# A hybrid decoder layer: the transposed keys are copied out of PSUM after the scores, and the idle products at the start read a smaller tile

## The chip, the cores and the metric

The kernel runs on one core of a Trainium2 chip. The metric is the device time of one execution in microseconds; before the change its median is 398.11 us in three runs (397.14 to 398.34).

## The reference, cut to what matters

One layer of a decoder, for 1024 prompt tokens and 64 sample tokens (8 sequences of 8), width 1024, float32. One input projection feeds two groups of heads; each is gated, both are concatenated, mapped by one output projection, and a layer norm ends the layer.

```python
proj = jnp.einsum('btd,de->bte', x, w_in)
u, gp, q, k, v, gg, fa = jnp.split(proj, SPLIT_IDX, axis=-1)
pool_out, new_buf = pool_mix(u, buf, start_pos, w_map, pool_scale)      # trailing windows 2/4/8/16
...
def step(S, inp):                                   # gated linear attention, one block of tokens
    qb, kb, vb, gb = inp
    b = jnp.cumsum(gb, axis=2)
    inter = jnp.einsum('bhck,bhkv->bhcv', qb * jnp.exp(b), S)
    ...
    A = jnp.einsum('bhtk,bhsk,bhtsk->bhts', qb, kb, decay)              # the scores, masked
    intra = jnp.einsum('bhts,bhsv->bhtv', A, vb)
    S_new = jnp.exp(bC)[..., None] * S + jnp.einsum('bhsk,bhsv->bhkv', kb * jnp.exp(bC[:, :, None] - b), vb)
    return S_new, inter + intra
...
mix = jnp.concatenate([pool_out * jax.nn.silu(gp), o.astype(x.dtype) * jax.nn.silu(gg)], axis=-1)
y = jnp.einsum('bte,ed->btd', mix, w_out)
h = (DEEPNORM_ALPHA * x + y).astype(jnp.float32)    # then the layer norm
```

## The kernel before

Every large product is taken three times over operands that are split into a rounded high part and a rest (`split`, lines 59 to 64; `mm3`, lines 66 to 70: high times high, high times rest, rest times high). The tokens stand in three pieces of 384, 384 and 320 columns.

The program has four stretches, each written out in the order in which the engines run it. First come the value projections (`v_group`, products named psv): the first three token tiles are worked with the contraction outermost, so that each piece of x and of the weights is used as soon as ScalarE and VectorE have split it (lines 309 to 318). Then 16 weight tiles, each over the three token pieces (`group`, products psm, 24 of them for one piece). After each piece `tick` runs what is due: `later` queues a step with a due slot, and slots count pieces. The steps of the gated linear attention are queued in this way (lines 432 to 440), one set for each of eight blocks of 128 prompt tokens (c = 0 to 7) and one for the 64 sample tokens (c = 8). Last come the output projection and the layer norm (`out_tile`, products pso).

For a prompt block c the steps due in one slot are, in this order: `s1a` of block c, `s2p` of block c-1, `s1b` of block c, `s2` of block c-1; `s3` of block c-1 follows one slot later. `s1a` transposes the keys of the block (two products pskt, line 724) into the first 256 columns of a PSUM bank called `pk`, and ScalarE copies them to SBUF as `kt` (line 726). `s2p` multiplies kt of the block before by its values (psp_, line 766). `s1b` computes the scores of the four heads (line 735): two heads go to the last 256 columns of the same bank (`pa[0]`, shown as pskt), two go to a second bank (psa). VectorE multiplies both by the mask into `am` (line 737). `s2` multiplies am of the block before by the values (line 804) and adds the queries times the state (line 802). `kt` of block c is read by `s2p` of block c one block later, and `am` of block c by `s2` of block c one block later. The squares of the output, their split and the sum over the ones (psms, line 833) follow in `s2` and `s3`. In the slot of block 0 there is no `s2p` and no `s2`, and in that of the sample block they are absent too.

Ahead of all this, GpSimd clears some tiles (lines 180 to 186), among them `warm`, 128 by 512; TensorE then multiplies this tile by itself nine times (line 189, psw), with a result that nobody reads, until the first pieces of x and of the weights are there. SyncE's queue issues the loads, the first at 0.73 us.

A second body, `Body(..., True)`, is run only when a flag says that the decay is too strong for the short form of the scores. It does not run with these inputs.

Of the kernel before, what the change touches and what calls it, by code (L numbers as in the profile page):

```python
# [7 lines left out]
F32 = mybir.dt.float32  # L8
FR = mybir.dt.float32r
I32 = mybir.dt.int32  # L10
ALU = mybir.AluOpType
AF = mybir.ActivationFunctionType
# [27 lines left out]
class Body:  # L40
# [54 lines left out]
    def emit(self):  # L95
        self.cms = {}
        tc, nc, io, safe = self.tc, self.nc, self.io, self.safe
# [32 lines left out]
        et = self.pool("et", 2)  # L130
# [46 lines left out]
                (nc.scalar if k == 0 and n == 0 else nc.sync).dma_start(raw, src)  # L177
        rst = ep.tile([128, 384], F32, name="rst")
        rst2 = ep.tile([128, 320], F32, name="rst2")
        nc.gpsimd.memset(wa2r, 0.0)  # L180
        nc.gpsimd.memset(sel, 0.0)
        nc.gpsimd.memset(eps[:, 0:1], RMS_EPS)
        nc.gpsimd.memset(eps[:, 1:2], LN_EPS)
        nc.scalar.preload_act_table_set(EXP_LN)
        warm = et.tile([128, 512], F32, tag="ab", name="warm")
        nc.gpsimd.memset(warm, 0.0)
        psw = psg.tile([128, 512], F32, tag="g", name="psw")
        for _ in range(9):
            nc.tensor.matmul(psw, warm[:, :128].bitcast(FR), warm.bitcast(FR), start=True, stop=True)  # L189


        order = [("k", 0), ("k", 1), ("q", 0), ("q", 1)]
# [362 lines left out]
        for j, t in enumerate(OUT_ORDER):  # L555
# [9 lines left out]
            if j in (4, 6):  # L565
                p = j // 2 - 2
# [115 lines left out]
    def gla_steps(self, c):  # L682
        nc, gl = self.nc, self.glp
        sample = c == 8
        t0, n = (128 * c, 128) if not sample else (NP, NS)
        K, Q = self.K[:, :, t0:t0 + n], self.Q[:, :, t0:t0 + n]
        msk = self.smask if sample else self.mask
        st = {}
# [3 lines left out]
        def g_tile(name):  # L692
            return self.psg.tile([128, 512], F32, tag="g", name=name)
# [14 lines left out]
        def s1():  # L708
            s1a()
            s1b()  # L710

        def s1a():
            Kst, Qi = K, Q
            am = gl.tile([128, 4, 128], F32, tag="am", bufs=1 if self.safe else 2, name="am")
            st["am"] = am
            if self.safe:
                Kst, Qi = self.safe_scores(c, am, t0, n, sample)
            st["Qi"] = Qi
            if sample and not self.safe:
                Kst = st["kd"]  # L720
            pk = g_tile("pskt")
            pa = [pk[:, 256:], None]
            for p in range(2):
                nc.tensor.transpose(pk[:n, p * 128:(p + 1) * 128], Kst[:, p], self.ident)
            kt = self.kt8 if sample else gl.tile([128, 256], F32, tag="kt", bufs=1 if self.safe else 2, name="kt")
            nc.scalar.activation(kt[:n], pk[:n, :256], AF.Copy)
            st["kt"], st["pa"] = kt, pa

        def s1b():
            am, pa, Qi = st["am"], st["pa"], st["Qi"]  # L730
            if not self.safe:
                pa[1] = g_tile("psa1")
                for h in range(4):
                    r, p = rows[h % 2], h // 2
                    nc.tensor.matmul(pa[h % 2][:n, p * n:(p + 1) * n], K[r, p], Q[r, p], start=True, stop=True)  # L735
                for e in range(2):
                    nc.vector.tensor_tensor(am[:n, two(e), :n], pa[e][:n, :2 * n].rearrange("s (p t) -> s p t", p=2),
                                            msk[:n, :n].unsqueeze(1).broadcast_to([n, 2, n]), op=ALU.mult)
            if sample:
                qb = gl.tile([128, 2, NB, 4, SEG], F32, tag="shl", bufs=1, name="qb")  # L740
                nc.gpsimd.memset(qb, 0.0)
                for p in range(2):
                    for h in range(2):
                        nc.vector.tensor_copy(qb[rows[h], p, :, h, :],
                                              Qi[rows[h], p].rearrange("k (b s) -> k b s", b=NB))
                st["qb"] = qb
# [108 lines left out]
        if sample:  # L855
            return [s0, s0k, s1, sample_inter, s2, s3]
        return [s1, s2, s3] if self.safe else [s1a, s1b, s2p, s2, s3]


# [174 lines left out]
```

## Time and profile before

| | us |
|---|---|
| median of three runs | 398.11 |
| the profiled execution | 397.98 |
| its span, first to last instruction | 396.2 |
| VectorE busy | 217.7 |
| ScalarE busy | 143.6 |
| values and gates, to about | 58 |
| first weight tiles, to about | 110 |
| weight tiles with the attention steps, to about | 222 |

A row of the timeline reads: start and duration in us, engine, line, operation, out<-in, the tile sizes, and in brackets the time that the engine stood idle before it with what released it. PE rows are TensorE's products, PEld rows are its weight loads, which run ahead of the products. A row of the view of waits reads: engine, what waited, line, what it waited for, then the time in total, how often, and the longest.

### The profile page before, as it was taken

To read this page: it belongs to the slowest core of one execution; us is meant where nothing else is said; L and a number is where in the kernel's file an instruction comes from. 1 tells how busy PE (TensorE), PEld (TensorE's weight loads), DVE (VectorE), ACT (ScalarE), POOL (GpSimd) and SP (SyncE) were. 2 spreads that over 40 slices of the span, in tenths; PEclk is the share of its full clock that TensorE was granted. 3 is DMA by queue.
4 is the path that set the end of the run, shared out by engine and by line. 5 is a ranking of instruction groups with operands and counts; after the bars stand their busy time and mean duration, and the time that the engine had idled before them with its cause. 6 is when DMAs were issued, how large, how long until landed. Compare 5 with 4: busy or idle time off the path is not lost.

```text
span 396.2 us, 6088 instructions
## 1 busy us (share of the span) xinstructions
PE 383.3 (97%) x2473; PEld 358.3 (90%) x2473; DVE 217.7 (55%) x429; ACT 143.6 (36%) x273; POOL 8.6 (2%) x31
## 2 busy tenths in 40 slices
PE   8999999999999999999999999999999999999991
PEld 7999999999989999999899899999988888888790
DVE  4775555621354778788433321333399565556683
ACT  5554554410023425435766222421283333211200
POOL 1000000000000000000001000100000000000000
PEclk9999999999999999999999999999999999999996
DMA  7960001011100101030103110443330253242321
GB/s 257 393 237 2 19 36 55 3 51 53 55 19 36 53 2 52 3 141 20 55 0 97 53 37 17 161 160 101 132 141 10 96 213 106 108 159 79 103 84 60
DMA packets 11556, 34.29 MB, mean 87 GB/s; under 512 B 1776, under 2 KB 3232, under 8 KB 11264
## 3 DMA queue, kind: packets, MB, share of 16 engines
q1 hardware_dynamic: 10960, 32.24, 23.7%
q0 software_dynamic: 416, 1.46, 1.1%
q8 instruction: 21, 0.34, 0.3%
q10 hardware_dynamic: 144, 0.14, 0.1%
q14 instruction: 15, 0.12, 0.1%
HBM read 27.91 MB, written 5.91 MB: 85 GB/s over the span
## 4 chain that ended last, share of the span: by engine, by line
PE 93%; ACT 3%; issue 1%; DVE 1%; POOL 0%; ACTq 0%; POOLq 0%
PE psm L68 15%; PE psm L69 15%; PE psm L70 15%; PE pso L68 7%; PE pso L69 7%; PE pso L70 7%; PE psv L69 4%; PE psv L68 4%; PE psv L70 4%; PE pskt L735 1%; PE psw L189 1%; PE pso L75 1%; PE pso L78 1%; PE pso L804 1%; PE psms L833 1%
## 5 line engine op out<-in xcount | busy, mean ns | idle before, releaser
L68 PE MATMUL psm<-xc,hl 128*128 128x384 f32 (+1 forms) x384 | 126.2, 329 | 0.0
L70 PE MATMUL psm<-xc,hl 128*128 128x384 f32 (+1 forms) x384 | 125.4, 327 | 0.0
L69 PE MATMUL psm<-xc,hl 128*128 128x384 f32 (+1 forms) x384 | 125.3, 326 | 0.0
L68 PEld LDWEIGHTS psm<-xc,hl 128*128 128x128 f32 x384 | 72.1, 188 | 0.7 <-issue 0.2
L69 PEld LDWEIGHTS psm<-xc,hl 128*128 128x128 f32 x384 | 72.2, 188 | 0.1
L70 PEld LDWEIGHTS psm<-xc,hl 128*128 128x128 f32 x384 | 72.1, 188 | 0.0
L68 PE MATMUL psv<-wv,xc 128*128 128x264 f32 x128 | 36.9, 288 | 0.0
L70 PE MATMUL psv<-wv,xc 128*128 128x264 f32 x128 | 36.7, 287 | 0.0
L69 PE MATMUL psv<-wv,xc 128*128 128x264 f32 x128 | 36.7, 286 | 0.0
L68 PE MATMUL pso<-wo,mx 128*128 128x512 f32 (+1 forms) x85 | 32.0, 377 | 0.0
L70 PE MATMUL pso<-wo,mx 128*128 128x512 f32 (+1 forms) x85 | 32.0, 377 | 0.0
L69 PE MATMUL pso<-wo,mx 128*128 128x512 f32 (+1 forms) x85 | 32.0, 377 | 0.0
L539 ACT ACTIVATE mv<-mv,eps 128x1 f32<-128x1 f32 (+1 forms) x9 | 2.7, 295 | 64.8 <-DVE mv L538 64.8
L403 DVE SCALAR_TENSOR_TENSOR vm<-sg,vecs,vm 128x128 f32<-128x128 f32 (+1 forms) x36 | 10.3, 340 | 27.8 <-ACT sg L397 27.8
L64 DVE TENSOR_TENSOR hl<-raw,hl 128x1024 fp32r<-128x1024 f32 x19 | 23.2, 1223 | 3.8 <-ACT hl L61 3.5
L644 ACT ACTIVATE ue<-psm 128x384 f32<-128x384 f32 (+1 forms) x12 | 5.5, 456 | 53.4 <-PE psm L70 49.5
L68 PEld LDWEIGHTS psv<-wv,xc 128*128 128x128 f32 x128 | 24.6, 192 | 0.1
L69 PEld LDWEIGHTS psv<-wv,xc 128*128 128x128 f32 x128 | 24.5, 191 | 0.1
L532 DVE SCALAR_TENSOR_TENSOR hh<-xr,pso 128x512 f32<-128x512 f32 (+2 forms) x19 | 12.4, 654 | 21.8 <-PE pso L70 21.6
L70 PEld LDWEIGHTS psv<-wv,xc 128*128 128x128 f32 x128 | 24.4, 190 | 0.0
L61 ACT ACTIVATE hl<-raw 128x1024 fp32r<-128x1024 f32 x19 | 19.9, 1051 | 6.4 <-PE psm L70 6.4
L68 PE MATMUL pso<-hl,mx 128*128 128x512 f32 (+1 forms) x51 | 19.3, 379 | 0.0
(236 smaller groups left out, 587.3 us busy)
## 6 DMA issues: line engine op xcount, KB each, us to landing
raw<-wm_dram SPq DMA_DIRECT2D x16, 512.0 KB, 3.5
xr<-x_dram SPq DMA_DIRECT2D x8, 512.0 KB, 4.3
o_y_dram<-hh SPq DMA_DIRECT2D x7, 512.0 KB, 2.9
wr<-w_out_dram SPq DMA_DIRECT2D x5, 512.0 KB, 4.5
s<-s_dram SPq DMA_DIRECT2D x2, 1024.0 KB, 6.7
hl<-xt_dram SPq DMA_DIRECT2D x2, 768.0 KB, 7.0
raw<-w_out_dram SPq DMA_DIRECT2D x3, 512.0 KB, 3.4
hl<-xt_dram SPq DMA_DIRECT2D x2, 640.0 KB, 5.4
```

The costliest lines, as they stand in the source:

```text
L61: self.nc.scalar.activation(hi.bitcast(FR), raw, AF.Copy)
L64: (on_lo or self.nc.vector).tensor_tensor(lo.bitcast(FR), raw, hi, op=ALU.subtract)
L68: nc.tensor.matmul(ps, ahi.bitcast(FR), bhi.bitcast(FR), start=first, stop=False)
L69: nc.tensor.matmul(ps, ahi.bitcast(FR), blo.bitcast(FR), start=False, stop=False)
L70: nc.tensor.matmul(ps, alo.bitcast(FR), bhi.bitcast(FR), start=False, stop=last)
L75: one = lambda st, sp: nc.tensor.matmul(ps, both.bitcast(FR), bhi.bitcast(FR), start=st, stop=sp)
L78: nc.tensor.matmul(ps[:64], both[:, :64].bitcast(FR), blo.bitcast(FR), start=False, stop=False)
L189: nc.tensor.matmul(psw, warm[:, :128].bitcast(FR), warm.bitcast(FR), start=True, stop=True)
L403: nc.vector.scalar_tensor_tensor(pg, sg[:, to:to + tn], self.norm[:, m:m + 1], pg, op0=ALU.mult, op1=ALU.mult)
L532: nc.vector.scalar_tensor_tensor(hh[:n, s], x[:n, s], ALPHA if n == 128 else 1.0, ps[h][:n, :wd], op0=ALU.mult, op1=ALU.add)
L644: nc.scalar.activation(ue[:, HIST:HIST + np_], src[:, :np_], AF.Copy)
L735: nc.tensor.matmul(pa[h % 2][:n, p * n:(p + 1) * n], K[r, p], Q[r, p], start=True, stop=True)
```

## The change

It has two parts. `warm` becomes 128 by 128, is cleared by GpSimd ahead of the other tiles, and the nine products read it four times over as a moving operand of 512 columns (an access that returns to the first column after each 128). And the copy of the transposed keys, `kt`, is taken out of `s1a` into a function `keys`, which `s1b` calls after the score products; in the second body it stays where it was.

```diff
         rst2 = ep.tile([128, 320], F32, name="rst2")
+        warm = et.tile([128, 128], F32, tag="ab", name="warm")
+        nc.gpsimd.memset(warm, 0.0)
         nc.gpsimd.memset(wa2r, 0.0)
         nc.gpsimd.memset(sel, 0.0)
         nc.gpsimd.memset(eps[:, 0:1], RMS_EPS)
         nc.gpsimd.memset(eps[:, 1:2], LN_EPS)
         nc.scalar.preload_act_table_set(EXP_LN)
-        warm = et.tile([128, 512], F32, tag="ab", name="warm")
-        nc.gpsimd.memset(warm, 0.0)
         psw = psg.tile([128, 512], F32, tag="g", name="psw")
+        wide = warm.bitcast(FR).unsqueeze(1).broadcast_to([128, 4, 128])
         for _ in range(9):
-            nc.tensor.matmul(psw, warm[:, :128].bitcast(FR), warm.bitcast(FR), start=True, stop=True)
+            nc.tensor.matmul(psw.rearrange("p (a c) -> p a c", a=4), warm.bitcast(FR), wide, start=True, stop=True)
...
             pk = g_tile("pskt")
-            pa = [pk[:, 256:], None]
+            pa = [pk[:, 256:], None, pk]
             for p in range(2):
                 nc.tensor.transpose(pk[:n, p * 128:(p + 1) * 128], Kst[:, p], self.ident)
+            st["pa"] = pa
+            if self.safe:
+                keys()
+
+        def keys():
             kt = self.kt8 if sample else gl.tile([128, 256], F32, tag="kt", bufs=1 if self.safe else 2, name="kt")
-            nc.scalar.activation(kt[:n], pk[:n, :256], AF.Copy)
-            st["kt"], st["pa"] = kt, pa
+            nc.scalar.activation(kt[:n], st["pa"][2][:n, :256], AF.Copy)
+            st["kt"] = kt
 
         def s1b():
             am, pa, Qi = st["am"], st["pa"], st["Qi"]
...
                     nc.tensor.matmul(pa[h % 2][:n, p * n:(p + 1) * n], K[r, p], Q[r, p], start=True, stop=True)
+
+                keys()
                 for e in range(2):
```

GpSimd's rows at the start of the program, before:

```order
L1009 UNCONDITIONAL_BRANCH [waits barrier_Pool_Activation_PE_DVE_SP_gather]
L180 MEMSET wa2r 128x256
L181 MEMSET sel 128x2
L182 MEMSET eps 128x1
L183 MEMSET eps 128x1
L186 MEMSET warm 128x512
L216 MEMSET fats 128x512
```

and of the change:

```order
L1017 UNCONDITIONAL_BRANCH [waits barrier_Pool_Activation_PE_DVE_SP_gather]
L181 MEMSET warm 128x128
L182 MEMSET wa2r 128x256
L183 MEMSET sel 128x2
L184 MEMSET eps 128x1
L185 MEMSET eps 128x1
L217 MEMSET fats 128x512
```

The clearing of warm has moved from fifth to first place behind the barrier and has a quarter of the columns.

TensorE's rows in the slot of block 3 (its transposes, the state product of block 2, the scores of block 3, then block 2's product with the old state), before, with the semaphores for which a row waits:

```order
L724 MATMUL pskt<-ident,K 128x128 [waits PE_49]
L724 MATMUL pskt<-ident,K 128x128
L766 MATMUL psp__1596<-vm,kt 64x128 [waits Activation_49]
L766 MATMUL psp__1596<-vm,kt 64x128 x3
L735 MATMUL pskt<-Q,K 128x128 [waits Activation_49]
L735 MATMUL psa_1602<-Q,K 128x128
L735 MATMUL pskt<-Q,K 128x128
L735 MATMUL psa_1602<-Q,K 128x128
L802 MATMUL psp__1596<-Q,S 128x128
L802 MATMUL pso_1609<-Q,S 128x128
```

and of the change:

```order
L725 MATMUL pskt<-ident,K 128x128 [waits PE_49]
L725 MATMUL pskt<-ident,K 128x128
L774 MATMUL psp__1594<-vm,kt 64x128 [waits Activation_49]
L774 MATMUL psp__1594<-vm,kt 64x128 x3
L741 MATMUL pskt<-Q,K 128x128
L741 MATMUL psa_1600<-Q,K 128x128 [waits Activation_49]
L741 MATMUL pskt<-Q,K 128x128
L741 MATMUL psa_1600<-Q,K 128x128
L810 MATMUL psp__1594<-Q,S 128x128
L810 MATMUL pso_1609<-Q,S 128x128 [waits Activation_49]
```

No product moves. The first score product no longer waits for ScalarE; the second one and the first product into pso now do. These two waits are for the ScalarE work that last read the bank that psa and pso take over (the logarithm over psms at line 837 and the copy of psmap at line 675, of the slot before; both lines as numbered before the change). They stood there before too, but the wait for the newer copy kt covered them.

VectorE's rows at the same place, before:

```order
L64 TENSOR_TENSOR pdhl<-pd,pdhl 128x320 [waits DVE_49]
L737 TENSOR_TENSOR am<-pskt,mask 128x2x128 [waits PE_49,Activation_49]
L737 TENSOR_TENSOR am<-psa_1602,mask 128x2x128 [waits PE_49]
L785 TENSOR_TENSOR S<-psp__1596,S 128x256 [waits PE_49]
L786 TENSOR_TENSOR S<-S,dec 128x256 [waits DVE_49]
```

and of the change:

```order
L64 TENSOR_TENSOR pdhl<-pd,pdhl 128x320 [waits DVE_49]
L745 TENSOR_TENSOR am<-pskt,mask 128x2x128 [waits Activation_49]
L745 TENSOR_TENSOR am<-psa_1600,mask 128x2x128 [waits PE_49]
L793 TENSOR_TENSOR S<-psp__1594,S 128x256 [waits PE_49]
L794 TENSOR_TENSOR S<-S,dec 128x256 [waits DVE_49]
```

The mask product over pskt waits for ScalarE's copy kt in both, since both read the same bank; the copy now itself waits for the last score product into that bank, so the wait for TensorE is covered by it. The order on ScalarE is the same as before.

## The prediction

> **What bounds the kernel now.** I read the engines' shares on the page first, then the shares of the chain that ended last, then TensorE's two rows in the view of waits and the one of its weight loads, and last the timeline at the places that these rows name.
>
> ```profile
> span 396.2 us, 6088 instructions
> PE 383.3 (97%) x2473; PEld 358.3 (90%) x2473; DVE 217.7 (55%) x429; ACT 143.6 (36%) x273; POOL 8.6 (2%) x31
> ...
> PE 93%; ACT 3%; issue 1%; DVE 1%; POOL 0%; ACTq 0%; POOLq 0%
> ```
>
> ```profile
> PE pskt L735 <- ACT kt L726: 1.9, 4, 0.6
> PE psw L189 <- POOL warm L186: 1.7, 1, 1.7
> ...
> PEld pskt L735 <- ACT kt L726: 4.5, 9, 0.9
> ```
>
> TensorE is on the chain for 93% of the span, so a microsecond that it does not stand is a microsecond of the time, unless something else comes late next. It stands for two things alone: the clearing of warm at the start, and the copy kt ahead of the scores. The change aims at exactly these. The weight loads show the stands in full (4.5 us in nine places); the products show 1.9, since their ends are modelled and cover the short ones.
>
> The time is summed against the profiled execution: 397.98 us, of which 396.2 are the span and 1.8 lie around it, which nothing here touches. That run is 0.13 under the median of 398.11.
>
> **First part: the scores no longer wait for kt.** One slot, block 3:
>
> ```profile
> 145.11 0.31 PEld L724 LDWEIGHTS pskt<-ident,K 128*128 128x128 f32 x2
> ...
> 145.59 0.42 PEld L766 LDWEIGHTS psp__1596<-vm,kt 128*64 128x64 f32 x8 [0.17 <-issue]
> ...
> 145.87 0.38 ACT L726 ACTIVATE kt<-pskt 128x256 f32<-128x256 f32 x1
> 146.30 0.18 PEld L735 LDWEIGHTS pskt<-Q,K 64*128 64x128 f32 x1 [0.29 <-ACT kt L726]
> ...
> 146.74 0.27 PE L735 MATMUL pskt<-Q,K 64*128 64x128 f32 x1
> ...
> 147.11 0.43 DVE L737 TENSOR_TENSOR am<-pskt,mask 128x256 f32<-128x256 f32 x1 [1.44 <-PE psa L735]
> ...
> 148.36 0.42 DVE L785 TENSOR_TENSOR S<-psp__1596,S 128x256 f32<-128x256 f32 x1 [0.49 <-PE psp__1596 L804]
> ```
>
> The copy ends at 146.25 and the first load for the scores starts at 146.30: 0.05 us from ScalarE to TensorE, and 0.29 of standing. The nine stands range from this 0.29 to 0.89; the large ones are in blocks 0 and 7 and in the sample block:
>
> ```profile
> 111.90 0.18 PEld L735 LDWEIGHTS pskt<-Q,K 64*128 64x128 f32 x1 [0.87 <-ACT kt L726]
> 196.51 0.18 PEld L735 LDWEIGHTS pskt<-Q,K 64*128 64x128 f32 x1 [0.70 <-ACT kt L726]
> 218.91 0.13 PEld L735 LDWEIGHTS pskt<-Q,K 64*64 64x64 f32 x1 [0.89 <-ACT kt L726]
> 208.09 0.18 PEld L802 LDWEIGHTS psp__2246<-Q,S 64*128 64x128 f32 x1 [0.17 <-issue]
> ```
>
> Not all of it goes. The last row is the slot in which the same psp_ products (tiles of 128 by 64) are followed by products of the scores' shape (64 by 128) with no copy to wait for, and the loads still stand 0.17 us; so do they between the transposes and psp_ in block 3. I take 0.17 as what a change of tile shape leaves at each of the nine places: 4.5 - 9 x 0.17 = **2.97 us saved**. From both sides: if it left nothing, 4.5; if the six small stands (0.29 to 0.44) gave nothing, the three large ones give 0.87 + 0.70 + 0.89 - 0.51 = 1.95. The slot of block 8 has the very sequence of blocks 1 to 7, so I stay with 2.97.
>
> [...]
>
> What the move costs elsewhere: kt now waits for the scores, and the mask product for kt. With a first load 0.12 earlier the scores of block 3 end at 146.89 instead of 147.01, kt runs from 146.94 to 147.32, and the mask starts near 147.4 instead of 147.11. Behind the mask on VectorE are the state products, which wait for TensorE's line 804 anyway (until 148.36); then on ScalarE the squares, and on TensorE psms one slot later. Behind kt on ScalarE is nothing due before these squares, but in block 0 and the sample block a weight split that is read a group later. The cover, where it is thin:
>
> ```profile
> 184.95 0.49 DVE L64 TENSOR_TENSOR pdhl<-pd,pdhl 128x320 fp32r<-128x320 f32 x1
> 185.84 0.19 PEld L68 LDWEIGHTS psmap<-pdhl,wmap 128*128 128x128 f32 x1
> ...
> 193.39 0.63 ACT L838 ACTIVATE rs<-rs 128x512 f32<-128x512 f32 x1
> 193.93 0.51 ACT L675 ACTIVATE pmix<-psmap,vecs 128x320 f32<-128x320 f32 x1
> ...
> 200.45 0.69 DVE L64 TENSOR_TENSOR sqhl<-sq,sqhl 128x512 fp32r<-128x512 f32 x1 [0.99 <-ACT sqhl L61]
> 202.60 0.36 PEld L833 LDWEIGHTS psms<-sqhl,ones 128*128 128x128 f32 x2
> ```
>
> In block 7 the split for psms is done at 201.14, 1.46 us ahead of its reader; a mask that is 0.3 late, and hidden behind line 804 besides, costs nothing. In block 6 the pool split is done 0.40 ahead of psmap (184.95 + 0.49 against 185.84), and its TensorE comes only 0.29 - 0.17 = 0.12 earlier. The two waits that come to light, of psa and pso, are for work done by 194.44 in block 7, where the scores come at about 196. If such a cover were gone, the price would be the lateness, a few tenths in one block. I add nothing.
>
> **Second part: the idle products start earlier.**
>
> ```profile
> 0.73 0.31 POOL L180 MEMSET wa2r<- 128x256 f32 x1 [0.29 <-POOLq L1030]
> 0.98 0.10 POOL L181 MEMSET sel<- 128x2 f32 x1
> ...
> 1.08 0.52 POOL L186 MEMSET warm<- 128x512 f32 x1
> ...
> 1.66 4.21 PE L189 MATMUL psw<-warm 128*128 128x512 f32 x9 [1.66 <-POOL warm L186]
> ...
> 4.39 0.51 ACT L61 ACTIVATE xc<-hl 128x384 fp32r<-128x384 f32 x1
> ...
> 4.93 0.56 DVE L64 TENSOR_TENSOR xc<-hl,xc 128x384 fp32r<-128x384 f32 x1
> ...
> 5.67 0.42 PE L68 MATMUL psv<-wv,xc 128*128 128x264 f32 x1
> ...
> 6.11 0.42 PE L70 MATMUL psv<-wv,xc 128*128 128x264 f32 x1
> ...
> 6.99 0.33 PE L68 MATMUL psv<-wv,xc 128*128 128x264 f32 x1
> ...
> 7.15 0.28 PE L69 MATMUL psv<-wv,xc 128*128 128x264 f32 x1
> 7.27 0.28 PE L70 MATMUL psv<-wv,xc 128*128 128x264 f32 x1
> ...
> 9.43 0.34 SPq L308 DMA_DIRECT2D wa2r<-w_a_dram  x1
> ```
>
> A clearing of 128 columns lies between those of 2 (0.10) and 256 (0.31); I take 0.20, so warm is there at 0.93 and the first idle product, 0.06 later as before (1.60 to 1.66), starts at **0.99, 0.67 earlier**. The nine then end 0.67 earlier, and the first real product could run at 5.00. It can't quite: the high part of x ends at 4.90, and the first product that reads the rest (line 70, at 6.11) needs VectorE's 5.49, plus 0.05 and one product step of 0.22 (5.67 to 6.11 in two steps): 5.76. So the real work moves by **0.35**.
>
> The step between products falls from 0.22 to 0.12 (7.15 to 7.27) at about 7.0, 5.3 us after the first idle product: the clock comes up. If it follows TensorE's own work it comes at 6.33. Real work 0.35 earlier at the slow step is worth 0.35 x 0.12 / 0.22 = 0.19, and the step 0.67 earlier 0.67 x (1 - 0.12 / 0.22) = 0.30: **0.49 us**. Nothing behind holds it up at first: the third piece of x is split only at 10.01 and read at 10.91:
>
> ```profile
> 9.05 0.96 DVE L64 TENSOR_TENSOR xc<-hl,xc 128x768 fp32r<-128x768 f32 x1 [0.60 <-ACT xc L61]
> ...
> 10.91 0.28 PE L70 MATMUL psv<-wv,xc 128*128 128x264 f32 x1
> ```
>
> That 0.9, less the hand-over, is also the most that an earlier start can bring: 0.85. The least is 0.19, with the clock unmoved. The other clearings come about 0.2 later; the first of them to be needed, wa2r, is loaded from 9.43 on.
>
> **Sum:** 397.98 - 2.97 - 0.49 = **394.5 us**, 0.9% under the median.
>
> **The rivals.**
>
> *The clock comes up by its own count, not by the idle products.* Then the step stays at 7.0 (0.19 instead of 0.49: 394.8) or falls ahead of the real work (0.85: 394.2). The one execution shown can't tell; runs that differ by 1.2 us speak for it. [...] 0.15.
>
> *The small stands give nothing*, because a change of shape costs more when the scores come straight behind psp_, or a thin cover like psmap's gives it back: 397.98 - 1.95 - 0.3 = 395.7. Against it is the 0.17 in block 8. 0.13.
>
> *The wait only changes its place*: the second score product now waits for ScalarE itself, and were that work late, the scores would stand as before and only the start would gain: 397.5. That work is over 1.5 us early in block 7. 0.05.
>
> *The repeated operand breaks the stream*, and this one ends slower. If the moving operand restarted at each of its four runs, each as an own 128-column product of 0.27 (the last score product above), an idle product would last some 1.1 even at the fast step, and the nine would reach from 0.99 to 10.9. Real work would start there. Before, seven products were issued by 7.15, worth 0.84 at the fast step, as if real work had begun at 6.3 at that step; so the loss is 10.9 - 6.3 = 4.6 and the time 397.98 - 2.97 + 4.6 = 399.6. It decides from 0.92 us for an idle product on: nine of these end at 9.3, where the loss equals 2.97. Against it:
>
> ```profile
> L189 PE MATMUL psw<-warm x9: 628/628/792, 1.7 to 5.2; 128*128 128x512 f32 x9
> ...
> 236.78 0.84 PE pso__2495 L810 x8
> ```
>
> The eight records at line 810 read the identity in four runs of 16 columns and take 0.1 each, far from four restarts. 0.03.
>
> **How the numbers follow.** The forecast as summed has 0.64, the others 0.15, 0.13, 0.05 and 0.03. Forecast, clock and small stands all lie more than 0.3% under the median (below 396.9; 0.3% is about what a measurement of this kernel can tell from no change): faster 0.92. Same 0.05, from the wait that changes its place; slower 0.03. The range runs from 393.2 (two thirds of the way to no loss at a change of shape, 4.5 saved, with the 0.85) to 396.2 (1.95 and 0.19 saved, and 0.4 for the scatter of the runs); it leaves out the last two cases and the far tails.
>
> **What would show it.** In the profile after, the waits no longer have a row of pskt for kt; the loads of the scores stand about 0.17 for issue at all nine places; the first idle product starts near 1.0 and the first line 70 near 5.8; the mask starts later against the scores by about 0.4, with no new row of TensorE waiting. The prediction is wrong if TensorE waits for psa, psms or psmap, if the scores stand 0.3 and more, or if the idle products take longer than 0.43 a piece.

## The result, and the profile after

The changed kernel takes **394.88 us** (median of 6 runs, 394.52 to 395.24); the kernel before, run beside it, 397.73 (6 runs, 397.14 to 398.34). The ratio is 0.9929, with a 95% interval of 0.9916 to 0.9942: 2.85 us faster, where 3.5 were forecast. Both predicted savings are there in the profile, and in this profile a little over half a microsecond is given back at a place of which the prediction doesn't speak, behind VectorE's last instruction.

The profile after was taken on an execution of 395.04 us. First the span, the engines' busy time and the chain that ended last:

```profile
span 393.1 us, 6078 instructions
...
PE 382.5 (97%) x2473; PEld 357.5 (91%) x2473; DVE 217.4 (55%) x429; ACT 144.4 (37%) x273; POOL 8.3 (2%) x31
...
PE 96%; DVE 1%; DMA 1%; ACT 0%; issue 0%
```

ScalarE's 3% of the chain have gone: the copies kt are no longer on it (2.7 us of it), nor is the ScalarE work that stood in front of them. In the view of waits (who waited for whom: us in all, times, the longest) these are the rows of the scores, the copy and the start:

```profile
DVE am L745 <- ACT kt L732: 9.3, 5, 4.3
...
ACT kt L732 <- PE psa L741: 6.4, 8, 1.0
...
PEld pskt L741 <- issue: 1.6, 9, 0.2
PE psw L190 <- POOL warm L181: 1.0, 1, 1.0
```

It is the copy that waits now, 6.4 us in all, and nobody waits for it who would set the time. TensorE's loads of the scores stand 1.6 us in nine places, for no other engine; before it was 4.5 us for kt. The saving there is **2.9 us**, where 2.97 were forecast. No row of TensorE waiting for psa, psms or psmap has come in.

The timeline of the slot of block 3, next (start, duration, engine and line):

```profile
143.68 0.42 PEld L774 LDWEIGHTS psp__1594<-vm,kt 128*64 128x64 f32 x8 [0.17 <-issue]
...
144.27 0.18 PEld L741 LDWEIGHTS pskt<-Q,K 64*128 64x128 f32 x1 [0.17 <-issue]
...
145.02 0.39 ACT L732 ACTIVATE kt<-pskt 128x256 f32<-128x256 f32 x1 [0.95 <-PE psa L741]
...
145.43 0.42 DVE L745 TENSOR_TENSOR am<-pskt,mask 128x256 f32<-128x256 f32 x1 [1.67 <-ACT kt L732]
```

Before the scores' first load TensorE stands 0.17 us, as it does before psp_, and as it did in block 8 before. The mask's first product starts 1.16 us behind that load (145.43 against 144.27), before it was 0.81 (147.11 against 146.30): 0.35 later against the scores, 0.4 were forecast.

And the timeline of the start:

```profile
0.73 0.20 POOL L181 MEMSET warm<- 128x128 f32 x1 [0.29 <-POOLq L1038]
...
0.99 4.20 PE L190 MATMUL psw<-warm 128*128 128x512 f32 x9 [0.99 <-POOL warm L181]
...
4.97 0.56 DVE L64 TENSOR_TENSOR xc<-hl,xc 128x384 fp32r<-128x384 f32 x1
...
5.00 0.40 PE L68 MATMUL psv<-wv,xc 128*128 128x264 f32 x1
...
5.59 0.39 PE L70 MATMUL psv<-wv,xc 128*128 128x264 f32 x1
...
9.11 0.96 DVE L64 TENSOR_TENSOR xc<-hl,xc 128x768 fp32r<-128x768 f32 x1 [0.48 <-ACT xc L61]
...
10.12 0.39 PE L70 MATMUL psv<-wv,xc 128*128 128x264 f32 x1
```

The clearing takes 0.20 us and the first idle product starts at 0.99, both as forecast. Nine idle products take 4.20 us, before 4.21: reading one tile four times over cost nothing here. The third piece of x is read at 10.12 instead of 10.91, 0.79 earlier, 0.05 us behind its split: more could not have come of the start.

So 0.79 + 2.92 = 3.71 us of work have gone by TensorE's last product, and the span is only 3.0 shorter. The rest shows behind VectorE's last instruction. This is its row, and SyncE's stores of the output, first before, then after:

```profile
389.86 1.41 DVE L546 SCALAR_TENSOR_TENSOR hh<-hh,mv,lng 128x512 f32<-128x512 f32 x2
...
390.63 1.92 SPq L548 DMA_DIRECT2D o_y_dram<-hh  x2
```

```profile
386.15 1.41 DVE L547 SCALAR_TENSOR_TENSOR hh<-hh,mv,lng 128x512 f32<-128x512 f32 x2
...
386.92 1.19 SPq L549 DMA_DIRECT2D o_y_dram<-hh  x2
```

From the end of that row to the end of the span it took 396.18 - 391.27 = 4.91 us, and now 393.14 - 387.56 = 5.58: 0.67 more. The sum closes with it: 397.98 - 3.71 + 0.67 + 0.1 (around the span) = 395.04. What these 0.67 us are became the main question.

### The profile page after: what moved, and what is told of

Same layout as the page of the kernel before. It is cut to its first block, busy times and chain, and to the rows that moved or that the text cites. A ratio compares the mean times of both kernels' runs of the same rounds, so it can differ in the third digit from the quotient of the medians.

```text
span 393.1 us, 6078 instructions
## 1 busy us (share of the span) xinstructions
PE 382.5 (97%) x2473; PEld 357.5 (91%) x2473; DVE 217.4 (55%) x429; ACT 144.4 (37%) x273; POOL 8.3 (2%) x31
## 4 chain that ended last, share of the span: by engine, by line
PE 96%; DVE 1%; DMA 1%; ACT 0%; issue 0%
PE psm L68 16%; PE psm L69 16%; PE psm L70 16%; PE pso L68 7%; PE pso L69 7%; PE pso L70 7%; PE psv L70 4%; PE psv L68 4%; PE psv L69 4%; PE pskt L741 1%; PE psms L841 1%; PE pso L75 1%; PE pso L78 1%; PE pso L812 1%; DMA raw<-wv_dram 1%; PE pss L603 1%
## 5 line engine op out<-in xcount | busy, mean ns | idle before, releaser
L68 PEld LDWEIGHTS psv<-wv,xc 128*128 128x128 f32 x128 | 24.1, 189 | 0.5 <-ACT xc L61 0.5
L70 PEld LDWEIGHTS psv<-wv,xc 128*128 128x128 f32 x128 | 24.0, 188 | 0.4 <-DVE xc L64 0.3
L69 PEld LDWEIGHTS psv<-wv,xc 128*128 128x128 f32 x128 | 24.1, 188 | 0.0
```

The costliest lines, as they stand in the source:

```text
L68: nc.tensor.matmul(ps, ahi.bitcast(FR), bhi.bitcast(FR), start=first, stop=False)
L69: nc.tensor.matmul(ps, ahi.bitcast(FR), blo.bitcast(FR), start=False, stop=False)
L70: nc.tensor.matmul(ps, alo.bitcast(FR), bhi.bitcast(FR), start=False, stop=last)
```

## The experiments

**Each part alone.** The change's two parts touch different lines, so each was put into the kernel before by itself.

In keys_only, in a block's preparation and behind its scores:

```diff
-            pa = [pk[:, 256:], None]
+            pa = [pk[:, 256:], None, pk]
...
+        def keys():
...
+                keys()
```

> The first part alone: the copy of the transposed keys stands behind the scores, the idle products as before. My theory: the nine stands ahead of the scores shrink from 4.5 us to 9 x 0.17 = 1.5, TensorE gets no new wait, and the time falls by 2.9 us against before (about 394.8 by the six runs' median of 397.7). If the start part carried much of the measured gain of 2.85, this would fall by only 2.0 to 2.4. If the end of the program gave part of the gain back by itself (in the profile the stretch from VectorE's last instruction to the end of the span grew from 4.9 to 5.5 us), it falls by about 2.3 and the stretch is again longer than before.

In warm_only, in the setup:

```diff
+        warm = et.tile([128, 128], F32, tag="ab", name="warm")
+        nc.gpsimd.memset(warm, 0.0)
...
+        wide = warm.bitcast(FR).unsqueeze(1).broadcast_to([128, 4, 128])
```

> The second part alone: a 128-column tile cleared first and read four times over, the copy of the keys as before. My theory: the first idle product starts at 1.0 instead of 1.66, and the gain hangs on when the clock comes up: 0.2 us with the clock where it was, 0.5 if it follows the idle products, at most 0.85; a median some 0.3 to 0.6 under before. Rival: the operands are the bound at the start, and the gain is under 0.2, no difference that can be measured. If the repeated operand were slower, the nine products would take longer than 4.2 us together.

keys_only takes 394.80 us (5 runs) against 397.70 of the kernel before on that chip: ratio 0.9919, interval 0.9906 to 0.9933. warm_only takes 397.23 (11 runs): 0.9987, interval 0.9978 to 0.9996, which is 0.16 to 0.87 us. Their waits, keys_only's first:

```profile
PE psw L189 <- POOL warm L186: 1.7, 1, 1.7
...
PEld pskt L740 <- issue: 1.6, 9, 0.2
```

```profile
PEld pskt L736 <- ACT kt L727: 4.5, 9, 0.9
...
PE psw L190 <- POOL warm L181: 1.0, 1, 1.0
```

Each part moves its own row and not the other's. The scores' part carries nearly the whole gain, and beside it the start's is hard to see: by the medians the parts gain 2.90 and 0.47, and the whole change, next on the same chip, 2.79. So they don't add visibly; the run-to-run spread of keys_only alone is 1.5. Nor do its five runs show the end's share, which by what was expected would have left a gain of 2.3, though in its profile the stretch behind VectorE's last instruction is longer (5.42 us).

**Both kernels once more**, unchanged, for their traces, since one profile of each can't tell how much at the start is chance.

> The whole change once more, on the same chip as its two parts. If the parts add, it lies under before by the sum of the two; the profile shows whether the clock again comes up ahead of the real products (step of 0.12 us at 5.0) and how long the stretch from VectorE's last instruction to the end of the span is this time. If that stretch is 4.9 rather than 5.5, the earlier value was chance.

> The kernel before, one look, for two places that vary without a cause in the program: when the step between products falls to 0.12 us (7.0 in the first profile) and how long the stretch after VectorE's last instruction is (4.9). If the clock counts by itself, the fall is at another time than 7.0, anywhere from about 3.6 to 7.0 and up; if it follows the idle products it is at 7.0 again.

The changed kernel takes 394.91 us (5 runs; ratio 0.9925), the kernel before 397.86 in its one run. There the fast clock comes at 7.02 us, after 7.06 in the first profile, which by itself speaks for a clock that follows the idle products; but keys_only and, further below, before_pad start them at 1.66 as well and have it at 5.84 and 5.54. In after_again the fast clock is there at 4.93 us, but the third piece of x is split only from 9.68 on and read at 10.69: this time it was the loads that held the start up. A third profile, with the last runs below, has 9.85, a little ahead of the 10.0 expected there. Over the nine profiles in which nine idle products start at 0.99 the third piece is read at 9.85 to 11.23, median 10.43; over the four in which they start at 1.66 at 10.21 to 10.91, median 10.83. So the earlier start is worth 0.4 us between the medians, where the readings of one group spread over 0.7 and 1.4.

**What sets the clock.** One idle product instead of nine; the other eight are left out.

```diff
-        for _ in range(9):
+        for _ in range(1):
```

> The changed kernel with one idle product instead of nine: the real work may start at the loads of x and of the weights, and the clock finds less work in front of it. Left out: eight idle products, whose output nothing reads. Theory A (the clock comes up at a time of its own after the first work, 3.9 to 5.7 us in the six profiles, idle or real work alike): the fast clock still comes 3.9 to 6.9 us behind the first idle product at 0.99, so at 4.9 to 7.9 us of the span; the real work starts at about 2 us if the loads allow it, or else waits for them; the time is within 1 us of the changed kernel's 394.9, since the idle products cover only time in which the loads are on their way. Theory B (the clock needs a row of work without a gap before it comes up): with gaps in the first 5 us it comes up later than 8 us, real work runs at the slow step until then, and the time is 395.9 to 397.5.

It takes 395.89 us (7 runs; before 397.53, ratio 0.9962, interval 0.9948 to 0.9975), 1.0 more than the changed kernel. Its timeline, where the step between products changes:

```profile
8.61 0.42 PE L68 MATMUL psv<-wv,xc 128*128 128x264 f32 x1
8.82 0.42 PE L69 MATMUL psv<-wv,xc 128*128 128x264 f32 x1
9.04 0.41 PE L70 MATMUL psv<-wv,xc 128*128 128x264 f32 x1
9.27 0.31 PE L68 MATMUL psv<-wv,xc 128*128 128x264 f32 x1
9.41 0.28 PE L69 MATMUL psv<-wv,xc 128*128 128x264 f32 x1
9.54 0.28 PE L70 MATMUL psv<-wv,xc 128*128 128x264 f32 x1
```

Steps of 0.22 become steps of 0.14 and 0.13 between 9.3 and 9.5; the trace's record of the clock has it at 9.30. That is 8.3 us behind the idle product and 4.3 behind the first real one (4.99): later than theory A allows, and slow as long as theory B has it. The first real product comes at 4.99 here and at 5.00 with nine idle products, so the other eight cover time in which the loads are on their way, and what they buy is the clock (9.30 here, 5.05 after).

In the traces' records the fast clock lasts 382.293 us in eleven of the fourteen profiles, whatever their spans (396.2 before, 393.1 after), 3.413 longer in pad9 and before_pad and 3.413 shorter in one_idle; 382.293 is 112 times 3.413. From these lengths the author estimates that the clock changes at marks 3.413 us apart; no trace shows a mark by itself. When the fast clock comes depends on the execution: mask_first and mask_again, the same kernel, have it at 6.5 and 4.8. Why the three profiles of the changed kernel (5.05, 4.93, 5.03) lie so close together, and the two of the kernel before, stays open. In the table a mark is the start of the fast clock or, where it says "stays slow", 3.413 us ahead of that start; next to it is the share of the 3.41 us ahead of the mark, its stretch, in which TensorE had work, idle products included:

| profile | first idle product | mark | share of work before it | clock there |
|---|---|---|---|---|
| before | 1.66 | 3.65 | 58% | stays slow, fast at 7.06 |
| warm_only | 0.99 | 3.32 | 68% | stays slow, fast at 6.73 |
| pad9_64 | 0.99 | 3.60 | 76% | stays slow, fast at 7.01 |
| pad9 | 0.99 | 3.82 | 83% | fast at 3.82 |
| after | 0.99 | 5.05 | 100% | fast at 5.05 |
| one_idle | 0.99 | 5.89 | 26% | stays slow, fast at 9.30 |

In the other eight profiles the clock came with the first stretch of 100%, and no stretch of 63% or less raised it. By these rows pad9_64's 76% left the clock slow and pad9's 83% raised it; that the share decides is the author's reading of them. It fits the rival "by its own count".

**Does the late mask cost anything?** The copy goes behind the mask's products.

```diff
-                keys()
                 for e in range(2):
...
+                keys()
```

> The changed kernel with the keys' copy put behind the two products of the mask instead of in front of them, so that the mask's products come about 0.4 us earlier against the scores and the keys' copy later. Theory of the prediction (that the mask comes later costs nothing, because what reads it has room): no wait of TensorE appears or goes in the blocks, the nine loads of the scores stay at about 0.2 us, and the time is that of the changed kernel, 394.9 within 0.4. Rival (the mask's lateness gives back part of the gain in some blocks): the time falls by 0.3 us or more, and VectorE's last instruction comes by as much earlier than in the changed kernel (387.6 and 388.1 us of the span in its two profiles).

It takes 394.38 us (4 runs; before 397.53, ratio 0.9919, interval 0.9902 to 0.9935), half a microsecond under the changed kernel's 394.9, as the rival would have it. But the gain doesn't come from the blocks: VectorE's last instruction ends 377.41 us behind the reading of the third piece of x, in the three profiles of the changed kernel 377.44 each. Here the copy waits for the mask, and TensorE stands no shorter:

```profile
ACT kt L732 <- DVE am L744: 14.4, 9, 3.0
DVE am L744 <- PE psa L741: 7.3, 3, 3.8
...
PEld pskt L741 <- issue: 1.6, 9, 0.2
```

So the mask's lateness costs nothing, and the half microsecond is at the end of the program.

**The end of the program.** The trace holds semaphore rows that the profile's views leave out. At the end all engines meet twice. In the profiles of the kernel before and of warm_only VectorE comes to the last meeting but one with the others; in the changed kernel it came 0.93 us behind the first of them, in after_again 0.41, in keys_only 0.88. What these have in common is a shorter VectorE program: the copy's new place saves it nine rows that only wait (546 of its rows in the trace of before, 537 after). Hence pad9, which puts nine rows back where they are never run.

```diff
             self.close("bs")
+            pad = self.flag.tile([1, 1], F32, name="pad")
+            for _ in range(9):
+                nc.vector.memset(pad, 0.0)
```

> The changed kernel with nine clears of one number by VectorE added behind its last instructions, in the second copy of the body, which is never run: VectorE's program becomes as long as that of the kernel before, and nothing that is executed is changed. Theory (the code of VectorE's last rows is fetched late, because the nine waits that went shifted its program against the pieces in which it is loaded): VectorE joins the last meeting of the engines together with the others again (in the three kernels with the keys behind the scores it came 0.92, 0.88 and 0.40 us behind the last of them, in the three others not), and the time is 0.4 to 0.9 us below the changed kernel's 394.9, at 394.0 to 394.5. Rival (the late joining comes with the order of the last work, not with the program's length): VectorE is late by 0.4 to 0.9 us as before, and the time stays at 394.9 within 0.3.

VectorE was in time, as the theory has it, but the kernel takes 395.95 us (6 runs), a microsecond more than without the rows. The two lines that follow are the products with wo by shape, of the changed kernel and of pad9 (count, busy us, mean ns of one):

```profile
L68 PE MATMUL pso<-wo,mx 128*128 128x512 f32 x75 | 29.2, 389 | 0.0
```

```profile
L68 PE MATMUL pso<-wo,mx 128*128 128x512 f32 x75 | 29.7, 396 | 0.0
```

They follow each other at 233 instead of 227 ns. pad9 was no clean experiment: its new tile moved the tiles laid out behind it by 32 bytes a partition, mx among them. So the rows were put in again without a tile, the opposite was tried (the kernel before, made as late as the changed one), and the yardstick and mask_first were run beside them on one chip.

For pad9_still on the changed kernel, and for before_pad, with range(131), on the kernel before:

```diff
             self.close("bs")
+            for _ in range(9):
+                nc.vector.memset(self.scale[0:1, 0:1], 0.0)
```

> The changed kernel once more, as the yardstick for the three runs beside it. 394.9 within 0.3, VectorE 0.4 to 0.9 us behind the other engines at the last meeting but one, and TensorE's first line 70 of the third piece of x no earlier than 10.0 us, at whatever time between 3.8 and 7 us the fast clock comes.

> The nine clears of the run pad9 again, but on a tile that is there already, so that no tile moves. VectorE's program has 1731 rows in the two bodies, where the changed kernel has 1723 and the kernel before 1732. Theory (a piece of VectorE's code is loaded late when its last rows lie just behind a boundary of the program): VectorE is in time at the last meetings, the products with wo take 389 ns as in the changed kernel, and the time is 0.4 to 0.9 us below that of after_third beside it. Rival (what cost 1 us in pad9 was the longer program and not the moved tiles): the products with wo take 396 ns again and the time is 395.9. Second rival (the late joining has to do with the order of work, and pad9 was in time by chance): VectorE is 0.4 us or more late, and the time is that of after_third within 0.3.

> The kernel before with 131 such clears behind the second copy of the body, which is never run: VectorE's program comes to 1851 rows, 128 more than the changed kernel's 1723, so that its last rows lie behind a boundary as there, if the boundary repeats every 64 or 128 rows. Theory: VectorE comes 0.4 to 0.9 us behind the others to the last meeting but one, as it never did in the kernel before, and the time is 0.3 to 0.9 us above that of the kernel before, at 398.0 to 398.5. Rival (late because of the keys' new place): VectorE is in time, and the time is that of the kernel before within 0.2.

> mask_first once more, beside the changed kernel on one chip. Its VectorE program has 1725 rows. If what it gained on the changed kernel (394.4 against 394.9) is the end of the program alone, VectorE is in time at the last meeting, its last instruction stands as far behind the first line 70 of the third piece of x as in after_third (377.4 us), and the time is within 0.3 of pad9_still's. If the mask's place gains by itself, that distance is 0.3 us or more shorter.

Times: after_third 394.93 us (394.05 to 394.99), pad9_still 394.36 (394.11 to 394.63), mask_again 394.36 (394.21 to 394.80), 5 runs each; before_pad 398.25 (12 runs) against the kernel before's 397.64 (17 runs), ratio 1.0017, interval 1.0007 to 1.0027. The end of the program in the profiles, in us of each span (rows are those of VectorE in the two bodies):

| profile | rows | VectorE's DRAIN | last 8 KB of code read | the others meet | VectorE joins |
|---|---|---|---|---|---|
| after | 1723 | 390.38 | 390.87 to 391.42 | 391.88 to 391.93 | 392.81 |
| after_third | 1723 | 389.61 | 390.10 to 390.53 | 391.40 to 391.45 | 391.92 |
| before_pad | 1851 | 393.35 | 393.85 to 394.36 | 394.84 to 394.89 | 395.66 |
| before | 1732 | 393.96 | 394.46 to 394.89 | 395.54 to 395.59 | 395.56 |
| pad9_still | 1731 | 390.28 | 390.77 to 391.34 | 392.08 to 392.12 | 392.09 |
| mask_again | 1725 | 390.56 | 391.34 to 391.65 | 392.06 to 392.11 | 392.08 |

The kernel before, with nothing but rows added that are never run, becomes late (0.82 behind the first of the others) and slower; the changed kernel with such rows comes in time. So the late joining hangs on the length of VectorE's program, and not on the keys. In the six profiles with 1723 or 1851 rows (these three, after_again, keys_only and one_idle) VectorE joins 2.24 to 2.43 us behind its DRAIN, 1.30 to 1.44 behind the end of the last code piece read, and one more piece is read 0.65 to 0.74 later, beyond the span's end. In the other eight profiles it joins with the others, and no such piece is read. The queue that reads these pieces (q14 of the page, "instruction", 8192 bytes a packet) has, in all fourteen profiles, one read each when VectorE has run 64, about 189, 317 and 445 of its rows (64, 190, 316 and 443 before, 64, 188, 317 and 448 after). From these steps of 124 to 131 rows the author estimates near 128 rows to a piece; before_pad, with 128 rows more than the changed kernel, became late. The queue reads at other times as well, 15 pieces within the span of after in all, and the trace doesn't say for which engine, so that the last piece is VectorE's is a reading, not shown. Not shown either, but in line with all this, is the theory of a row which stands just behind the edge of a piece and is fetched only when VectorE comes to it. How far the bad lengths reach (1725 is good already) was not tried out.

How much it costs differs by execution. The stretch from the first engines' meeting to the span's end is 0.64 us in each of the eight profiles in which VectorE is in time. In the six others it is longer by all but 0.31 us of the lateness, which lies beside work that GpSimd does between the two meetings: by 0.10, 0.21 and 0.62 in the three of the changed kernel, by 0.41, 0.50 and 0.57 in one_idle, before_pad and keys_only, 0.40 in the mean. So 0.62 of the 0.67 us in question are VectorE's lateness. By the device times it is less sure: the 16 runs of the changed kernel have a mean of 394.8, the 14 of mask_first, mask_again and pad9_still 394.4; on the one chip the difference is 0.57 between the medians but 0.2 between the means, with overlapping runs.

**The moved tiles.** The last run moved the tiles by 64 bytes instead of 32.

```diff
-            pad = self.flag.tile([1, 1], F32, name="pad")
+            pad = self.flag.tile([1, 16], F32, name="pad")
```

> The run pad9 with a new tile of 64 bytes a partition in place of 4: the tiles behind it, which pad9 moved by 32 bytes, are moved by 64. wo, the streamed operand of the products that were slow there, is in its old place in both; mx, their stationary one, and the tiles that VectorE and ScalarE write meanwhile are moved. Theory (the place within 64 bytes decides: in the changed kernel mx begins 32 bytes behind a multiple of 64, in pad9 at one, here 32 behind one again): the products with wo take 389 ns again, VectorE is in time at the last meeting, and the time is that of pad9_still, 394.4 within 0.3. Rival (any distance from the old place slows them, for instance against wo's fixed place): 396 ns and 395.9.

It takes 396.83 us (10 runs; before 397.54), and the products with wo are slow again, in this kernel's rows by shape:

```profile
L68 PE MATMUL psm<-xc,hl 128*128 128x384 f32 x256 | 86.7, 339 | 0.0
...
L69 PE MATMUL pso<-wo,mx 128*128 128x512 f32 x75 | 29.6, 394 | 0.0
```

So it isn't the place within 64 bytes, and the theory falls. pad9_still, with 389 ns in these products and 337 in the upper group, has the rows and not the tile, and mask_first, on pad9's chip, has 389 ns: what was slow is the tiles' place. In pad9 the 225 products with wo, 6.6 ns longer each by their step, make 1.5 of the 1.6 us; in pad9_64 they leave about 1 us of the 2.5 unexplained. By what rule the place counts stays open.

## Why the prediction held, and where it was short

- **The stands of the scores** (2.97 us). Right: 4.5 us of waiting for kt became 1.6 us in which no other engine was waited for, at the change of shape in all nine places, 0.17 each and 0.20 in the sample block. The rows of block 8 and of psp_ gave the price of the case that the profile of before did not show. The rival in which the small stands give nothing is out (the 0.3 in its sum of 395.7 isn't worked out there).
- **Lateness of the copy and the mask** (0). Right in size, and shown by mask_first and mask_again: with the mask in front of the copy VectorE's last instruction ends at the same distance from the start, 377.41 and 377.43 against 377.44. The wait didn't change its place either.
- **The start** (0.49). The first idle product came at 0.99 to the hundredth, and the repeated operand cost nothing (4.20 us for nine, 4.21 before). What failed is the step "if it follows TensorE's own work it comes at 6.33": the clock came at 5.05, 4.93 and 5.03 in the changed kernel's profiles, 4.06, 3.94 and 4.04 behind the first idle product, where before it was 5.40. The real work also moved further than 0.35: the first line 70 ran at 5.59 and not at 5.76, 0.06 behind the split of x. The product step of 0.22 that the sum puts between the two wasn't there, nor was it with the clock still slow (in warm_only 5.55 behind 5.48). The profiled gain was 0.79, near the bound of 0.85 set by the split of the third piece. That is the second branch of the rival "by its own count" (394.2 there). As a mean over executions, 0.49 was a fair size (0.4 between the medians of the third piece's reading, 0.16 to 0.87 by the runs of warm_only), but by luck: it was worked out with a clock that follows the idle products.
- **"1.8 lie around it, which nothing here touches"** and, unsaid, that the end of the program stays as it is. Here the sum was short: a term for the end is missing from it. In the profiled pair the distance from VectorE's last instruction to the span's end grew by 0.67 us, 0.62 of it by VectorE's late joining. That VectorE's program loses nine waiting rows could be seen ahead, since the order shows the waits; that its length could cost time could not be read from the profile of before, where VectorE joins in time.

The forecast of 394.5 missed by 0.4 us, about what the end gives back (0.10 to 0.62 in the changed kernel's profiles). Without that, pad9_still and mask_first run at 394.4.

## What to carry to other kernels

A stand that ends with the releaser's work isn't all to be had: look for the same pair of neighbours elsewhere in the trace with nothing to wait for, and subtract what they stand there (here 0.17 us stayed at eight of the nine places, 0.20 at the sample block). When work vanishes on the path and the time doesn't follow, compare the distance from the last work to the end of the span before looking at the middle (here 4.91 us became 5.58). And an edit meant to change nothing, a few rows that never run or a tile of four bytes, was worth half a microsecond or more either way here (pad9_still 0.57 us under after_third, before_pad 0.61 above the kernel before, pad9 1.6 above pad9_still), so an experiment that adds one needs its own control.

## What the runs showed beyond that

- The fast clock lasted 382.293 us in eleven of the fourteen profiles and 3.413 more or less in three, and the same kernel had it at 4.8 and at 6.5 us; by the author's estimate of the marks, a stretch with work in 83% of it raised the clock (pad9), one with 76% did not (pad9_64).
- VectorE came 0.41 to 0.93 us late to the engines' last meeting but one in the six profiles with 1723 or 1851 rows in its program, and all but 0.31 us of that was added to the span; with 2 to 9 rows more than in the changed kernel (mask_first and mask_again, pad9_still, the kernel before) it was in time, and with 128 more (before_pad) 0.82 late.
- Moving tiles by 32 or 64 bytes slowed the products with wo from 389 to 396 and 394 ns, and the kernel by 1.6 and 2.5 us against pad9_still, which has its tiles in place.
